# A recurrence over sixteen heads: four groups one after the other, or all keys first and one chain

## The chip, the cores and the metric

The kernel runs on one core of a Trainium2 chip. A core has a matmul engine (PE, with a separate weight load, PEld), a vector engine (DVE), a scalar engine (ACT), a general engine (POOL), a queue engine (SP) and sixteen DMA engines. The engines run side by side; each takes its own instructions in the order in which the built program has them, and waits on semaphores for what others make. Matmuls read SBUF and write PSUM (eight banks of 128 partitions by 512 fp32). The metric is the device time of one execution in microseconds (us): three runs of the kernel before took 1127.19, 1123.43 and 1123.09, median 1123.43.

## The reference

One layer of a hybrid trunk over 512 tokens of width 1024 in fp32. The input is normalized and projected to 11,520 columns, out of which three mixers work:

```
y_a = b_a * causal_dwconv(c_a * x_a)                    # short gated convolution
y_b = rg_lru(causal_dwconv(x_b)) * gelu(g_b)            # linear recurrence, element by element
# RWKV-7: 16 heads of 64, state (64 x 64) per head, over the tokens in order:
state = state * w_t + (state @ -kk_t) (kk_t * a_t)^T + v_t k_t^T
y_t   = state @ r_t
yc    = groupnorm(y) * lnx_g + lnx_b + bonus;  y_c = yc * g_c
m = gate_a * y_a + gate_b * y_b + gate_c * y_c
x = x + m @ w_out;   x = x + relu(rms(x) @ w1)^2 @ w2;   return rms(x)
```

The change concerns the RWKV-7 recurrence and how m is put together; mixers a and b, the projections, the output projection and the MLP compute the same.

## The kernel before, in words

**Matmuls.** Every large product keeps fp32 accuracy by splitting both operands into a rounded part and a rest: mm3 (lines 162 to 165) issues three matmuls of 128x128 against 512 columns (hi x hi, hi x lo, lo x hi). A weight block (128 x 1024) comes by SP's queue into raw (2 buffers); ACT casts it to whi (line 142) and DVE subtracts the rest, wlo (through the helper tt, line 99), each with 3 buffers. One projection is 24 large matmuls, and it needs one such split from DVE.

**The recurrence.** The tokens are cut into 8 chunks of 64, and the 16 heads into 4 groups of 4. For a group:
- krv (385) makes keys, receptances and values from six projections, with some fifteen DVE operations of 512 columns per half group, into AR, BK, v and bv.
- amat (461) makes the masked products of keys inside each chunk: pA matmuls (two of the four heads use the lower 64 rows, two the upper), multiplied by a mask into AXt (DVE, 8 times 512 columns), and transposes of BK (pB).
- inverse (488) inverts the unit triangular matrices of 32 (chunk, head) pairs. DVE transposes AXt into Z, makes 31 steps of two dependent operations (dg<-Z, Z<-Z,dg, 31 to 256 columns on 64 partitions) and transposes back, last into dg. From dg PE makes the off-diagonal blocks (pG, then pT, 32 small matmuls each, with a copy by ACT after each).
- chain (539) carries the state over the chunks. In a chunk: pu = AXt x sv, copied to u0; pu = TT x u0, copied to sv; pS = BKT x sv, which with the old state gives the new one; py = RT x state + AXt x sv, the output, copied to Y. Each step is one 64x64 matmul for each of the group's 4 heads, fp32.
- post (646) and post_norm (609) normalize Y, transpose it (pYt), multiply it by the gate's projection and send it to DRAM (mpd).

**What sets the order.** A scheduler orders every engine's instructions by priority; `tc.high_priority(offset)` moves a piece ahead. weave (752) steps through a critical generator, each piece at the offset CP = 150 (CPI = 60, CPP = 30 where the generator asks for it), and for every step takes r steps of a fill generator. Fill is ab(q) (660), the mixers a and b for 128 of the 1024 channels, eight projections each, and krv of the next group. fill_main (771) lets krv(g + 1) begin only when the inverse of group g is done:

```
        while not GS[g].inv_done:
            yield
        b = krv(g + 1, GS[g + 1])
```

So four times in a row stand: amat and inverse with ab as fill; chain and post with krv of the next group and the rest of ab. The last group's chain has the output projection w_out as fill: w_out(th) for one half of the tokens (256 columns) needs m for that half. pin (167) only keeps matmuls that must not trade places in program order. ab reads the group's y_c back from mpd, adds, splits m into mh and ml and (for six of the eight) sends both to DRAM; open_m fetches them at the end.

After that come the MLP's two products (from line 908), which the change leaves as they are.

## Time and profile before

| | |
|---|---|
| median of three runs | 1123.43 us |
| the profiled execution | 1124.29 us, span 1122.5 us, granted clock 0.986 |
| PE busy | 1086.3 us (97%), 6396 records |
| DVE busy | 762.5 us (68%) |
| ACT busy | 507.5 us (45%) |
| POOL busy | 67.0 us (6%) |
| DMA | 118.8 MB, mean 106 GB/s |

A PE record's duration reaches from its start to the end of its way through the array, so records overlap, and the distance between starts is what one costs. An fp32 matmul is two records. A line number such as L99 or L102 is that of a helper; the names of the tiles tell the operation. The idle time of an engine that nothing waits for costs nothing. A row of the stretches gives the busy time of each engine in a piece of the span.

### The profile page before, as it was taken

To read this page: it belongs to the slowest core of one execution; us is meant where nothing else is said; L and a number is where in the kernel's file an instruction comes from. 1 tells how busy PE (TensorE), PEld (TensorE's weight loads), DVE (VectorE), ACT (ScalarE), POOL (GpSimd) and SP (SyncE) were. 2 spreads that over 40 slices of the span, in tenths; PEclk is the share of its full clock that TensorE was granted. 3 is DMA by queue.
4 is the path that set the end of the run, shared out by engine and by line. 5 is a ranking of instruction groups with operands and counts; after the bars stand their busy time and mean duration, and the time that the engine had idled before them with its cause. 6 is when DMAs were issued, how large, how long until landed. Compare 5 with 4: busy or idle time off the path is not lost.

```text
span 1122.5 us, 16257 instructions
## 1 busy us (share of the span) xinstructions
PE 1086.3 (97%) x6396; PEld 868.4 (77%) x6396; DVE 762.5 (68%) x1367; ACT 507.5 (45%) x826; POOL 67.0 (6%) x108
## 2 busy tenths in 40 slices
PE   8899989999989999989999989999999999999997
PEld 4677867778867778867778867898888888888885
DVE  7998995889975889975888957686444443222224
ACT  6555355534456534466534464555334433111214
POOL 2300000000001000001000020100000000000001
PEclk9899998999999999999999999999999999999999
DMA  6242223231233231233231263454332335333221
GB/s 209 74 122 74 72 85 96 65 114 57 91 118 104 75 118 57 89 115 114 73 109 57 85 189 121 171 175 165 101 104 94 94 94 188 99 104 97 94 94 75
DMA packets 38988, 118.80 MB, mean 106 GB/s; under 512 B 4736, under 2 KB 8320, under 8 KB 38912
## 3 DMA queue, kind: packets, MB, share of 16 engines
q1 hardware_dynamic: 30624, 95.21, 26.7%
q0 software_dynamic: 7568, 21.50, 6.3%
q8 instruction: 50, 0.82, 0.3%
q10 hardware_dynamic: 720, 1.05, 0.3%
q14 instruction: 26, 0.21, 0.1%
HBM read 104.64 MB, written 8.91 MB: 101 GB/s over the span
## 4 chain that ended last, share of the span: by engine, by line
PE 70%; DVE 23%; issue 3%; ACT 2%; DMA 1%; SPq 0%; ACTq 0%; DVEq 0%
PE pp L163 8%; PE pp L165 8%; PE pp L164 8%; PE acc L164 6%; PE acc L165 6%; PE acc L163 6%; PE p L165 5%; PE p L163 5%; PE p L164 5%; DVE wlo L99 5%; DVE dg L99 4%; DVE Z L99 3%; DVE u L102 2%; PE pA L471 2%; DVE g L102 2%
## 5 line engine op out<-in xcount | busy, mean ns | idle before, releaser
L99 DVE TENSOR_TENSOR wlo<-raw,whi 128x1024 fp32r<-128x1024 f32 (+1 forms) x172 | 209.5, 1219 | 216.6 <-ACT whi L142 214.3
L142 ACT CAST whi<-raw 128x1024 fp32r<-128x1024 f32 (+1 forms) x172 | 178.1, 1036 | 284.1 <-PE acc L165 125.1
L165 PE MATMUL pp<-hh,wlo 128*128 128x512 f32 x696 | 278.4, 401 | 5.8 <-DVE wlo L99 5.8
L164 PE MATMUL pp<-hl,whi 128*128 128x512 f32 x696 | 277.5, 399 | 3.2 <-DVE hl L102 3.2
L163 PE MATMUL pp<-hh,whi 128*128 128x512 f32 x696 | 279.3, 402 | 1.4 <-DVE ks L102 0.6
L165 PEld LDWEIGHTS pp<-hh,wlo 128*128 128x128 f32 x696 | 131.9, 190 | 34.8 <-DVE wlo L99 7.4
L163 PEld LDWEIGHTS pp<-hh,whi 128*128 128x128 f32 x696 | 132.1, 190 | 32.2 <-ACT u L664 2.1
L164 PEld LDWEIGHTS pp<-hl,whi 128*128 128x128 f32 x696 | 132.0, 190 | 30.6 <-DVE hl L102 4.3
L165 PE MATMUL p<-h2h,wlo 128*128 128x512 f32 (+1 forms) x264 | 101.2, 383 | 0.0
L163 PE MATMUL p<-h2h,whi 128*128 128x512 f32 (+1 forms) x264 | 101.1, 383 | 0.0
L164 PE MATMUL p<-h2l,whi 128*128 128x512 f32 (+1 forms) x264 | 101.0, 383 | 0.0
L163 PE MATMUL acc<-whi,ah 128*128 128x512 f32 x256 | 99.6, 389 | 0.0
L164 PE MATMUL acc<-wlo,ah 128*128 128x512 f32 x256 | 99.6, 389 | 0.0
L165 PE MATMUL acc<-whi,al 128*128 128x512 f32 x256 | 99.6, 389 | 0.0
L165 PEld LDWEIGHTS p<-h2h,wlo 128*128 128x128 f32 x264 | 49.6, 188 | 9.7
L164 PEld LDWEIGHTS p<-h2l,whi 128*128 128x128 f32 x264 | 49.6, 188 | 9.7
L163 PEld LDWEIGHTS p<-h2h,whi 128*128 128x128 f32 x264 | 49.6, 188 | 9.5
L164 PEld LDWEIGHTS acc<-wlo,ah 128*128 128x128 f32 x256 | 48.0, 188 | 10.1
L165 PEld LDWEIGHTS acc<-whi,al 128*128 128x128 f32 x256 | 48.0, 188 | 10.0
L163 PEld LDWEIGHTS acc<-whi,ah 128*128 128x128 f32 x256 | 48.0, 188 | 9.9
L99 DVE TENSOR_TENSOR Z<-Z,dg 64x31 f32<-64x31 f32 (+15 forms) x124 | 42.2, 340 | 4.1
L99 DVE TENSOR_TENSOR dg<-Z 64x31 f32<-64x31 f32 (+15 forms) x124 | 42.2, 340 | 4.1
(297 smaller groups left out, 1525.0 us busy)
## 6 DMA issues: line engine op xcount, KB each, us to landing
raw<-in_win SPq DMA_DIRECT2D x88, 512.0 KB, 3.5
raw<-in_w SPq DMA_DIRECT2D x64, 512.0 KB, 3.5
raw<-in_wout SPq DMA_DIRECT2D x16, 512.0 KB, 3.5
swr<-in_sw SPq DMA_DIRECT2D x16, 128.0 KB, 2.1
RT<-AR POOLq DMA_DIRECT2D x4, 512.0 KB, 5.4
AXt<-AR POOLq DMA_DIRECT2D x8, 256.0 KB, 5.0
x2T<-in_xt POOLq DMA_DIRECT2D x4, 512.0 KB, 7.1
x2d<-st POOLq DMA_DIRECT2D x8, 256.0 KB, 2.7
```

The costliest lines, as they stand in the source:

```text
L99: return v.tensor_tensor(out=o, in0=a, in1=b, op=op)
L102: return v.scalar_tensor_tensor(out=o, in0=a, scalar=s, in1=b, op0=op0, op1=op1)
L142: ac.copy(hi[:, sl], raw[:, sl])
L163: pe.matmul(ps, wh, xh, start=start, stop=False)
L164: pe.matmul(ps, wh, xl, start=False, stop=False)
L165: pe.matmul(ps, wl, xh, start=False, stop=stop)
L471: pe.matmul(pts[h][:, ci], G_.BK[rows, jj, c], G_.AR[rows, jj, c], start=True, stop=True)
```

## The change

The recurrence is taken in two phases.

**Phase one** goes through the four groups with krv, amat and inverse alone. krv(g) now runs side by side with inverse(g - 1) as one critical stream, with ab(0) to ab(5) as fill (0.60 fill steps to a step). Nothing of a group stays in SBUF for the chain: AR, AXt, BKT, TT and the transposed values are stored by POOL's queue into five DRAM tensors, laid out by chunk (axd, bkd, rtd, ttd, vtd). amat writes to four PSUM banks, the three of the chain and one of pm, and its matmuls alternate between lower and upper rows.

**Phase two** is one chain of eight chunks in which every step has 16 matmuls, for all 16 heads. load_chunk fetches a chunk's operands one chunk ahead (five DMAs on POOL's queue: sv 256 KB, ax 1 MB, tc 256 KB, bk 512 KB, rt 256 KB). The copies between steps are 512 columns wide, one half by DVE and one by ACT. After every second chunk norm treats Y for all heads, 1024 columns at once. Fill is what is left of ab, then gate(q), which prepares for each q a factor GQ and an addend BV such that m = GQ x norm + BV; fin_m applies them to a half of the tokens for all eight q and splits the result, between the gates and w_out(0), and again between w_out(0) and w_out(1). The trips of mh and ml through DRAM are gone. pin now puts all but the first matmul of a step far ahead (HOT = 6000), so that a step's matmuls stand together.

Three places show it, as the program's order has them; the first column is the source line.

PE in the chain before, group 0 (pu, pS and py are the chain's matmuls, pp those of a projection):

```order
L563 MATMUL pu<-sv,AXt 64x64 x4
L165 MATMUL pp<-hh,wlo 128x512
L163 MATMUL pp<-hh,whi 128x512
L164 MATMUL pp<-hl,whi 128x512
L571 MATMUL pu<-u_1554,Z 64x64 x4
L578 MATMUL py<-St,RT 64x64 x4
L165 MATMUL pp<-hh,wlo 128x512
L163 MATMUL pp<-hh,whi 128x512
L593 MATMUL pS<-sv,BKT 64x64 x4
L578 MATMUL py<-sv,AXt 64x64 x4
L164 MATMUL pp<-hl,whi 128x512
```

Each step is four matmuls between two to three large ones.

PE in the chain now, second chunk:

```order
L166 MATMUL pp<-hh,whi 128x512
L632 MATMUL pu<-sv,ax 64x64 x16
L167 MATMUL pp<-hl,whi 128x512
L168 MATMUL pp<-hh,wlo 128x512
L166 MATMUL pp<-hh,whi 128x512
L167 MATMUL pp<-hl,whi 128x512
L168 MATMUL pp<-hh,wlo 128x512
L166 MATMUL pp<-hh,whi 128x512
L167 MATMUL pp<-hl,whi 128x512
L652 MATMUL pu<-u_4737,tc 64x64 x4
L642 MATMUL py<-St,rt 64x64 x16
L652 MATMUL pu<-u_4737,tc 64x64 x12
```

A step's four matmuls have become sixteen, with the projections' matmuls between steps as before.

DVE in the inverse of group 0 before (dg and Z are the inverse's two operations of a step, wlo the weight split):

```order
L99 TENSOR_TENSOR dg<-Z 64x156
L99 TENSOR_TENSOR Z<-Z,dg 64x6x26
L99 TENSOR_TENSOR dg<-Z 64x175
L99 TENSOR_TENSOR Z<-Z,dg 64x7x25
L99 TENSOR_TENSOR dg<-Z 64x192
L99 TENSOR_TENSOR Z<-Z,dg 64x8x24
L99 TENSOR_TENSOR dg<-Z 64x207
L99 TENSOR_TENSOR Z<-Z,dg 64x9x23
L99 TENSOR_TENSOR dg<-Z 64x220
L99 TENSOR_TENSOR Z<-Z,dg 64x10x22
L99 TENSOR_TENSOR wlo<-raw,whi 128x1024
L99 TENSOR_TENSOR dg<-Z 64x231
```

Between the inverse's steps stands a split now and then.

The same place on DVE now (ks, rqw and rqq, a and bl belong to krv of the next group):

```order
L105 SCALAR_TENSOR_TENSOR ks<-pp,part,ks 128x511
L102 TENSOR_TENSOR Z<-Z,dg 64x5x27
L102 TENSOR_TENSOR dg<-Z 64x156
L102 TENSOR_TENSOR Z<-Z,dg 64x6x26
L102 TENSOR_TENSOR dg<-Z 64x175
L102 TENSOR_TENSOR Z<-Z,dg 64x7x25
L102 TENSOR_TENSOR bl<-a_1105,bh 128x512
L102 TENSOR_TENSOR dg<-Z 64x192
L102 TENSOR_TENSOR Z<-Z,dg 64x8x24
L192 STREAM_TRANSPOSE rqw<-pn 128x512
L102 TENSOR_TENSOR wlo<-raw,whi 128x1024
L195 TENSOR_SCALAR rqq<-rqw 128x16
```

The next group's keys have moved in between the same steps.

DVE at the norm of the last chunks before (gst and Y are the norm, x2T and h2l the output projection):

```order
L102 SCALAR_TENSOR_TENSOR gst<-gst 128x8 x2
L99 TENSOR_TENSOR x2T<-acc,x2T 128x256
L99 TENSOR_TENSOR gst<-gst 128x8
L102 SCALAR_TENSOR_TENSOR gst<-gst 128x8 x2
L99 TENSOR_TENSOR gst<-gst 128x8
L102 SCALAR_TENSOR_TENSOR gst<-gst 128x8
L99 TENSOR_TENSOR wlo<-raw,whi 128x1024
L102 SCALAR_TENSOR_TENSOR gst<-gst 128x8
L102 SCALAR_TENSOR_TENSOR h2l<-x2T,part,h2h 128x256
L99 TENSOR_TENSOR Y<-Y,gst 128x512
L99 TENSOR_TENSOR x2T<-acc,x2T 128x256
L99 TENSOR_TENSOR wlo<-raw,whi 128x1024
```

The norm of one group alternates with the output projection's work.

The same place on DVE now:

```order
L102 TENSOR_TENSOR wlo<-raw,whi 128x1024
L691 TENSOR_REDUCE gst<-ysq 128x16
L102 TENSOR_TENSOR wlo<-raw,whi 128x1024
L105 SCALAR_TENSOR_TENSOR h2l<-x2T,part,h2h 128x256
L108 TENSOR_SCALAR gst<-gst 128x16 x2
L102 TENSOR_TENSOR gst<-gst 128x16
L105 SCALAR_TENSOR_TENSOR gst<-gst 128x16 x2
L102 TENSOR_TENSOR gst<-gst 128x16
L105 SCALAR_TENSOR_TENSOR gst<-gst 128x16 x2
L102 TENSOR_TENSOR gst<-gst 128x16
L105 SCALAR_TENSOR_TENSOR gst<-gst 128x16 x2
L102 TENSOR_TENSOR Y<-Y,gst 128x1024
```

The norm's operations are twice as wide and stand closer together.

PE just behind that norm now (pYt are the transposes of Y, acc the output projection):

```order
L166 MATMUL acc<-mh,whi 128x256
L167 MATMUL acc<-ml,whi 128x256
L168 MATMUL acc<-mh,wlo 128x256
L702 MATMUL pYt<-ident,Y 128x128 x8
L166 MATMUL acc<-mh,whi 128x256 x2
L167 MATMUL acc<-ml,whi 128x256
L168 MATMUL acc<-mh,wlo 128x256
L166 MATMUL acc<-mh,whi 128x256
L167 MATMUL acc<-ml,whi 128x256
L168 MATMUL acc<-mh,wlo 128x256
L167 MATMUL acc<-ml,whi 128x256
L168 MATMUL acc<-mh,wlo 128x256
```

The transposes that need the norm stand ahead of the second half of the output projection.

The diff, cut to its core:

```
...
+CP, CPI, CPC, CPN = 150, 60, 70, 5
+HOT = 6000
+R0, R1, R2, R3, R4 = 0.85, 0.60, 1.25, 3.9, 1.0
-HEADS = ((0, 1), (0, 0), (1, 1), (1, 0))
+HEADS = tuple((x, h) for x in range(8) for h in (1, 0))
...
+    def pin(n, mm):
+        if not n:
+            mm()
+            return
+        with tc.high_priority(offset=HOT):
+            m = mm()
+        if m is not None:
+            tc.keep_in_program_order(m)
...
+    def amat(g, G_):
+        G_.AX = p1.tile([P, 2, NC, 4, L], F32, tag="AXt", name="AXt")
+        for c4 in range(2):
+            pts = four_banks("pA")
+            for i in range(16):
+                ci, jj, h = i // 4, i // 2 % 2, i % 2
+                c = 4 * c4 + ci
+                rows = slice(64 * h, 64 * h + 64)
+                pin(i, lambda: pe.matmul(pts[2 * h + jj][:, ci], G_.BK[rows, jj, c], G_.AR[rows, jj, c],
+                                 start=True, stop=True))
+            for e in range(4):
+                tt(G_.AX[:, :, 4 * c4:4 * c4 + 4, e], pts[e].rearrange("p c (a t) -> p a c t", a=2),
+                   mask.rearrange("p (a t) -> p a t", a=2).unsqueeze(2).to_broadcast([P, 2, 4, L]), MUL)
...
+    def load_chunk(c):
...
+        gp.dma_start(flat(sv[64:128]), flat(vtd[c]))
+        gp.dma_start(flat(ax), flat(axd[c]))
+        gp.dma_start(flat(tc_), flat(ttd[c]))
+        if c < NC - 1:
+            gp.dma_start(flat(bk), flat(bkd[c]))
+        if c > 0:
+            gp.dma_start(flat(rt), flat(rtd[c]))
...
+            for n, (x, h) in enumerate(HEADS):
+                g, e = x // 2, 2 * h + x % 2
+                pin(n, lambda: pe.matmul(pu[64 * h:64 * h + 64, x], ax[rows, g, 0, e], sv[rows, g, e],
+                                 start=True, stop=True))
+            u0 = C["ph2"].tile([L, NG, 4, L], F32, tag="u0", name="u0")
+            v.tensor_copy(u0[:, :, 0:2], by_tile(pu[0:64]))
+            ac.copy(u0[:, :, 2:4], by_tile(pu[64:128]))
...
+            if c % 2 == 1:
+                yield CPN
+                norm(c - 1, c + 1)
...
+    def fin_m(c_lo, c_hi):
+        n, th = c_hi - c_lo, c_lo // 4
+        for g in range(NG):
...
+            for h in range(2):
+                q = 2 * g + h
+                y = C["ph2"].tile([P, HT], F32, tag="ym", name="ym", bufs=2)
+                tt(y.rearrange("p (c t) -> p c t", t=L), pt[:, 0:n, 64 * h:64 * h + 64],
+                   GQ[q][th].rearrange("p (c t) -> p c t", t=L), MUL)
+                tt(y, y, BV[q][th], ADD)
+                GQ[q][th], BV[q][th] = gq_tile(q, th, F32R), bv_tile(q, th, F32R)
+                ac.copy(GQ[q][th], y)
+                tt(BV[q][th], y, f(GQ[q][th]), SUB)
...
+    fl = chainit(*[ab(q) for q in range(6)])
+    weave(chainit(krv(0, GS[0]), amat(0, GS[0])), fl, R0)
+    for g in range(1, NG):
+        weave(chainit(side_by_side(krv(g, GS[g]), inverse(g - 1, GS[g - 1])), amat(g, GS[g])), fl, R1)
+    weave(inverse(NG - 1, GS[NG - 1]), fl, R2)
...
+    fc = fill_chain()
+    weave(chain(), fc, R3)
+    weave(end(), fc, R4)
```

More of the change, by code (lines that the diff above doesn't have):

```diff
@@ L382, in block_kernel @@
     class G:
-        inv_done = False
+        pass
     def krv(g, G_):
@@ L525, in inverse @@
             yield
+        for _ in range(NG_T):
+            yield CPI
         for half in range(2):
@@ L834, in last_fill, with fill_chain @@
+    def fill_chain():
+        yield from fl
+        for q in (6, 7):
+            yield from ab(q)
+        for q in range(KT):
+            yield from gate(q)
         wk_ctx.close()
@@ L887, in to_tokens, with end @@
                 yield
-    def post_half(th):
-        yield from post_norm(NG - 1, G_, 4 * th, 4 * th + 4)
-        if th == 0:
-            M["half"] = True
-    fl = last_fill()
-    segments([(chainit(amat(G_), inverse(G_), open_m()), R4),
-              (chainit(chain(G_, 0, 4), post_half(0), chain(G_, 4, NC), post_half(1)), R5)], fl)
-    drain(fl)
-    fin_m(1)
+    def end():
+        while "half" not in M:
+            yield
+        yield from fin_m(4, 8)
+    fc = fill_chain()
+    weave(chain(), fc, R3)
+    weave(end(), fc, R4)
+    drain(fc)
     drain(to_tokens(0))
```

407 lines of the change are left out of this document (176 added, 231 removed).

## The prediction

> **What bounds the kernel now.** I read the page's busy shares first (PE 97%), then cut the span at the marks that the change moves. The stretches below end, in turn, at the last pA matmul of a head group, at its first pG matmul, and so on for four groups (106.8 to 655.4), then at the first matmul of the output projection (703.4) and of the first MLP product (762.8). Columns: length, then busy time and instructions of PE, PEld, DVE, ACT, POOL, granted clock, DMA share, GB/s.
>
> ```profile
> 0.00:106.80 106.80, 97.11 (x408) 71.92 (x409) 91.98 (x176) 62.24 (x94) 18.08 (x26) 0.95 0.39 123
> 106.80:160.10 53.30, 53.30 (x243) 43.50 (x241) 50.49 (x92) 21.57 (x30) 0.56 (x1) 1.00 0.23 74
> 160.10:254.90 94.80, 89.79 (x746) 67.17 (x746) 74.20 (x155) 47.66 (x91) 6.35 (x11) 0.95 0.30 90
> 254.90:338.40 83.50, 79.48 (x347) 64.08 (x345) 73.21 (x119) 42.24 (x61) 2.36 (x6) 0.98 0.31 96
> 338.40:424.30 85.90, 85.48 (x746) 64.21 (x746) 66.32 (x146) 43.11 (x86) 6.82 (x11) 1.00 0.29 90
> 424.30:506.20 81.90, 77.89 (x347) 62.92 (x345) 72.88 (x119) 42.01 (x61) 2.36 (x6) 1.00 0.30 93
> 506.20:592.30 86.10, 86.10 (x749) 64.50 (x748) 66.52 (x147) 42.90 (x86) 6.70 (x10) 1.00 0.30 93
> 592.30:655.40 63.10, 59.49 (x262) 47.85 (x261) 59.04 (x102) 28.27 (x41) 1.72 (x4) 0.97 0.26 81
> 655.40:703.40 48.00, 47.74 (x427) 35.88 (x427) 28.32 (x61) 29.22 (x53) 8.45 (x15) 1.00 0.53 158
> 703.40:762.80 59.40, 59.20 (x561) 55.44 (x561) 45.89 (x98) 33.06 (x66) 5.09 (x8) 1.00 0.54 178
> 762.80:1122.50 359.70, 350.74 (x1578) 290.96 (x1576) 133.65 (x157) 115.22 (x162) 8.55 (x10) 0.99 0.33 107
> sum 1122.50, PE 1086.32 PEld 868.42 DVE 762.51 ACT 507.51 POOL 67.04; mean PE 98.76 PEld 78.95 DVE 69.32 ACT 46.14 POOL 6.09
> ```
>
> PE sets the time almost everywhere; it lacks work for 36 us, 9.7 of them before 106.8 and 9.0 after 762.8, which the change leaves. In the chain stretches (338.4 to 424.3, 506.2 to 592.3) PE never waits. In the inverse stretches (those that end at 160.1, 338.4, 506.2 and 655.4) DVE is busy 88 to 95%, and in the last three PE loses 3.6 to 4 us each; 5 more go right after the first. So two things can be won, PE's own overheads and those waits, and one can be lost: DVE is the engine next in line.
>
> **Fewer runs of small matmuls.** PE's cost of leaving a projection for a run of 64x64 matmuls and coming back:
>
> ```profile
> 204.82 0.39 PE L165 MATMUL pp<-hh,wlo 128*128 128x512 f32 x1
> 205.14 0.45 PE L563 MATMUL pu<-sv,AXt 128*64 128x64 f32 x8
> 205.52 0.50 PE L163 MATMUL pp<-hh,whi 128*128 128x512 f32 x1
> 205.85 0.39 PE L164 MATMUL pp<-hl,whi 128*128 128x512 f32 x1
> 206.08 0.40 PE L165 MATMUL pp<-hh,wlo 128*128 128x512 f32 x1
> ```
>
> A row counts records, two for an fp32 matmul. An undisturbed 128x512 matmul is issued every 0.23 us (205.85 to 206.08). From 204.82 to 205.85 are 1.03 us, of which two such take 0.46 and the eight small records, four matmuls, about 0.28 (the row's 0.45 less most of the pipeline's tail); the remaining 0.3 us is the price of a run. Counted in the order, small matmuls stand in 165 runs before and in 85 after, with as many of each matmul as before. 80 x 0.3 = **24 us of PE time removed**.
>
> **pA in pairs.** The mask products' matmuls use 64 of the 128 rows each. Where the old order happened to alternate the two halves they ran together:
>
> ```profile
> L471 PE MATMUL pA<-AR,BK 64*128 64x128 f32 x256 | 27.9, 285 | 0.9 <-DVE AXt L99 0.8
> 245.88 1.16 PE L471 MATMUL pA<-AR,BK 64*128 64x128 f32 x8
> 248.09 1.49 PE L471 MATMUL pA<-AR,BK 64*128 64x128 f32 x16
> ```
>
> Sixteen records took 0.33 us more than eight. The new order alternates strictly, so at best half of 27.9 goes; some was paired already. I take 11 us (bounds 0 and 14), 2.8 a group. Against it, the four multiplies that free the four banks stand before the second sixteen: about 1 us of wait a group.
>
> **DVE in phase one.** This is the term that decides. The old kernel held krv of the next group back until the inverse was done; now both run together, so DVE's queue between the first transposes of AXt and the last transpose that pG waits for holds far more. Prices:
>
> ```profile
> L99 DVE TENSOR_TENSOR wlo<-raw,whi 128x1024 fp32r<-128x1024 f32 (+1 forms) x172 | 209.5, 1219 | 216.6 <-ACT whi L142 214.3 <-ACT rs L296 1.2
> L99 DVE TENSOR_TENSOR dg<-Z 64x31 f32<-64x31 f32 (+15 forms) x124 | 42.2, 340 | 4.1
> L99 DVE TENSOR_TENSOR AXt<-pA,mask 128x512 f32<-128x512 f32 x32 | 20.9, 686 | 9.3 <-PE pA L471 9.1
> L495 DVE STREAM_TRANSPOSE Z<-AXt 32x1024 f32<-32x1024 f32 x8 | 16.6, 2078 | 0.2
> L517 DVE STREAM_TRANSPOSE dg<-Z 32x1024 f32<-32x1024 f32 x4 | 4.9, 1225 | 0.0
> 729.69 1.22 DVE L99 TENSOR_TENSOR wlo<-raw,whi 128x1024 fp32r<-128x1024 f32 x1
> 730.83 0.68 DVE L618 TENSOR_REDUCE gst<-ysq 128x8 f32<-128x512 f32 x1
> ```
>
> The order of the change has there, for group 0: the 62 operations of the inverse's steps (62 x 0.34 = 21.1), five transposes (4 x 2.08 + 1.2 = 9.5), 11 weight splits (13.4), 48 operations of 512 columns (at 0.7, near the 0.686 of AXt: 33.6), and small change by the same view, 3 scans (3.7), 24 operations of 128x16 (4.1) and one of 256 (0.4): 85.8. An operation that doesn't need its predecessor starts 0.08 before that one's recorded end (729.69 + 1.22 against 730.83); some 80 such neighbours take off 6.4. With the four AXt multiplies ahead (2.7) DVE has **82 us** from the last pA to pG. Groups 1 and 2, counted alike (12 and 10 splits), have 86 and 82.5. PE's work between the same marks is 332, 308 and 330 large matmuls x 0.227 plus 6 to 8 runs and 24 transposes (near a pA record's 27.9 / 256 = 0.11 each): **80, 74 and 79 us**. Before, it was 223 large ones against 6 splits and 13 wide operations. So DVE's queue is now the longer one. Where the two were level before (592.3 to 655.4) each was busy 94% of the stretch. At that share the stretches take 87, 91.5 and 88 us; the lower bound is DVE without a gap (82, 86, 82.5), the upper the 88% that DVE reached in 254.9 to 338.4 (93, 98, 94). I take the 94%, the row of level loads. After pG, up to the next group's last pA, PE leads:
>
> ```profile
> 338.51 2.14 PE pG L522 x64
> ```
>
> 100, 93 and 48 large matmuls, pG and pT (2.14 each), 4 to 5 runs and pA (6.9 less 2.8, plus 1 of wait) make 33, 31.5 and 21 us. The last inverse has 6 splits, 12 wide operations and one of 256 beside its own 30.6: 49 with AXt, against 179 large matmuls (43 with their runs); 50. Up to the first last pA nothing moves but the pairing: 105.5.
>
> Phase one thus ends at 105.5 + 87 + 33 + 91.5 + 31.5 + 88 + 21 + 50 = **507.5 us**, some 40 us (7 + 17.5 + 9 + 7) more than PE's own work would need. The saving on runs is spent on waiting for DVE.
>
> **The chain.** From there to the output projection: 580 large matmuls (131.7), 652 small ones (at some 0.06, a little under the 0.28 / 4 above: 39) in 23 runs (6.9), about 177 in all; the old stretches took 1 to 2% more than such counts give, so 180. The start waits for the last TT to be stored and for the first loads, behind 55 projection matmuls (12.5 us) in PE's order.
>
> ```profile
> x2T<-in_xt POOLq DMA_DIRECT2D x4, 512.0 KB, 7.1
> ```
>
> A store and a 1 MB load after it, each near these 7 us, make 14 and issue time: 2 us late, bounds 0 and 8. Later loads (2.3 MB a chunk, one chunk ahead, over 20 us apart) raise the traffic from about 90 to some 190 GB/s, which the queues carried at a share of 0.54 (178 GB/s in 703.4 to 762.8): hidden by the projections; without that cover each would cost its 7 to 10 us. Chain steps have 7 to 24 large matmuls behind which to hide; I add 2 for chunk 1, where only two stand between py and pu. Sum 184. The copies and the state update shrink DVE's work there, which costs or wins nothing while PE leads.
>
> **The output projection.** The chain now ends inside it. In PE's order 61 matmuls of 256 columns (7.3 us at the 0.12 between the first two rows below) stand between the last py and the transposes pYt that need the norm of the last two chunks. The norm took before, hidden behind other such matmuls:
>
> ```profile
> 728.35 0.28 PE L164 MATMUL acc<-ml,whi 128*128 128x256 f32 x1
> 728.47 0.28 PE L165 MATMUL acc<-mh,wlo 128*128 128x256 f32 x1
> 727.53 0.27 ACT L605 COPY Y<-py 128x128 f32<-128x128 f32 x1 [2.07 <-PE py L578]
> 737.88 0.65 PE L627 MATMUL pYt<-ident,Y 128*128 128x128 f32 x4
> L99 DVE TENSOR_TENSOR x2T<-acc,x2T 128x256 f32<-128x256 f32 x16 | 6.7, 421 | 5.2 <-PE acc L165 4.9
> ```
>
> From Y to pYt is 10.3 us for half the width; four passes of DVE and two of ACT over twice the columns add 3. So 13.3 - 7.3 = 6 us of wait, with all of w_out's second half queued behind pYt. Then fin_m runs for eight heads' tiles, not two: 24 operations of 256 columns (at x2T's 0.42, 10 us), twice, against three weights' 8.6 us of matmuls whose buffers it holds; 3 us each time with the restart. In sum 56.4 of work + 12 = 68.5, against 59.4.
>
> **Sum.** 507.5 + 184 + 68.5 + 359.7 = 1119.7 of span. The profiled execution took 1124.29 for its 1122.5, that is 1.8 more, and the median of the runs is 0.9 below it: **1120.5 us**, 0.3% under before, which is no change: a run of this kernel can't tell less than about 0.5%. Its own range is 1110 to 1130.
>
> **Rivals.**
>
> *DVE keeps up.* If the splits run far enough ahead, or the dependent steps of the inverse fill each other's gaps, PE waits no more than before, and the removed 24 + 11 us stay less the 12 at the end: 1124.3 - 35 + 12 = 1101, **1100** as a median. For it: before, PE waited only 4 us in stretches with DVE at 88%. Against it: the counts above, 82 to 86 against 74 to 80.
>
> *The clock falls.* Slower than before. The waits come in one piece at pG, at the chain's start and at pYt, and PE is granted half its clock after each:
>
> ```profile
> 163.40:168.40 5.00, 0.47 (x3) 0.04 (x1) 4.31 (x6) 4.95 (x8) 1.77 (x3) 0.78 0.40 94
> 168.40:172.00 3.60, 3.57 (x65) 3.51 (x65) 3.48 (x5) 2.53 (x3) 0.00 (x0) 0.50 0.84 231
> 172.00:175.60 3.60, 3.60 (x17) 2.43 (x16) 0.00 (x0) 1.33 (x4) 0.57 (x1) 0.50 0.58 216
> 484.00:488.00 4.00, 1.53 (x7) 0.96 (x6) 3.27 (x5) 0.85 (x2) 0.00 (x0) 1.00 0.38 82
> 488.00:492.00 4.00, 3.78 (x16) 2.86 (x17) 3.21 (x4) 3.28 (x5) 0.00 (x0) 1.00 0.50 167
> ```
>
> After 4.5 us without work the clock stood at 0.50 for 7.2 us, 3.6 lost; after 2.5 us it stayed at 1.00. It decides once gaps in one piece are longer than a point that lies between these two; five of them cost 18: 1120.5 + 18 = **1138.5**. Against it: waits spread over many splits leave the clock alone. The Trainium skill ("TensorE: Matmul & The Clock Gate", Part 1: The HAM clock gate) says that PE falls to half its rate after an idle window of about 3.4 us and needs as long a busy one to return; the trace agrees on the rate (0.50).
>
> **Numbers.** Forecast 0.52 (of it 0.17 under 1117.8, 0.30 within 0.5%, 0.05 over 1129), DVE keeps up 0.25, the clock falls 0.23. Faster 0.42, same 0.30, slower 0.28. The DVE stretches' bounds alone give 1104 to 1139; with the first rival and a little past the second the range is 1100 to 1142.
>
> **What would show it.** 85 runs, and PE free of waits in the chain: the first term. pA busy near 15 us: the second. From last pA to pG near 88 us with DVE at 94% and PE short of work by 6 to 8 us: the third; were PE full there, the first rival holds. A gap of about 6 us before pYt: the last. Wrong altogether if the chain stretch takes much over 184 us (loads late) or the clock's mean falls well under 0.986.

## The result: 3.3% slower

| | before | after |
|---|---|---|
| median beside each other on one chip | 1123.26 us | 1161.15 us (4 runs, 1157.73 to 1165.03) |
| ratio | | 1.033 [1.029, 1.0375] |
| the profiled execution, its span | 1124.29, 1122.5 us | 1160.24, 1158.1 us |
| granted clock | 0.986 | 0.959 |
| PE busy, PE idle | 1086.3, 36.2 us | 1073.4, 84.7 us |
| DVE, ACT, POOL busy | 762.5, 507.5, 67.0 us | 758.3, 484.8, 108.6 us |
| DMA | 118.8 MB | 146.3 MB |

The span grew by 35.6 us: PE is busy 12.9 us less and idle 48.5 us longer. The stretches of the changed kernel, cut at the same marks as in the prediction (the last pA matmul of a group, its first pG, and so on; then the first matmul of the output projection and of the MLP), with the same columns:

```profile
0.00:104.60 104.60, 93.91 (x410) 69.16 (x410) 87.47 (x175) 61.95 (x94) 25.42 (x34) 1.00 0.43 135
104.60:202.10 97.50, 86.58 (x367) 68.78 (x365) 91.60 (x170) 40.32 (x59) 8.91 (x14) 0.93 0.42 115
202.10:233.90 31.80, 31.80 (x286) 26.44 (x286) 16.88 (x24) 15.16 (x20) 2.88 (x5) 1.00 0.37 109
233.90:327.30 93.40, 81.70 (x342) 64.62 (x339) 89.44 (x167) 40.40 (x59) 10.73 (x17) 0.93 0.41 111
327.30:358.30 31.00, 30.34 (x279) 25.08 (x279) 13.40 (x19) 11.23 (x16) 2.05 (x4) 1.00 0.40 120
358.30:463.70 105.40, 86.80 (x365) 68.76 (x363) 91.47 (x169) 42.52 (x62) 11.83 (x18) 0.90 0.39 108
463.70:487.40 23.70, 23.44 (x234) 18.86 (x234) 12.71 (x20) 12.33 (x19) 1.09 (x2) 0.86 0.29 73
487.40:539.90 52.50, 43.23 (x201) 35.43 (x200) 49.63 (x93) 23.80 (x34) 4.66 (x7) 0.95 0.48 132
539.90:730.40 190.50, 187.24 (x1872) 153.72 (x1872) 118.54 (x206) 90.59 (x136) 27.56 (x51) 0.96 0.57 183
730.40:799.40 69.00, 58.34 (x490) 56.12 (x491) 54.25 (x111) 32.25 (x58) 5.44 (x9) 0.90 0.45 149
799.40:1158.10 358.70, 350.01 (x1572) 290.34 (x1570) 132.88 (x157) 114.25 (x159) 8.02 (x9) 0.99 0.33 107
```

The span lies 38.4 us above the predicted 1119.7, and 32.4 of them arise in phase one: it ends at 539.9, and the prediction had 507.5. The four inverse stretches (97.5, 93.4, 105.4, 52.5) hold 10.9, 11.7, 18.6 and 9.3 us without PE, and the granted clock is down in each.

PE's waits of the changed kernel (engine, line, what was waited for: us in total, times, longest):

```profile
PE pA L522 <- DVE BK L102: 13.9, 3, 4.8
PE pp L166 <- DVE ks L105: 10.2, 3, 7.0
PE pG L576 <- DVE dg L571: 9.0, 1, 9.0
PE pYt L702 <- DVE Y L102: 8.6, 1, 8.6
PE pp L166 <- DVE v L105: 5.5, 1, 5.5
PE pn L431 <- ACT bh L161: 3.7, 1, 3.7
```

The line of the same view before that holds its longest single wait:

```profile
PE pT L530 <- ACT dg L524: 4.6, 1, 4.6
```

BK, ks, v and bh belong to krv of the next group, dg is the last transpose of an inverse, Y the last norm. PE waits not only at the ends of DVE's queue, where the prediction looked, but in the middle. One such place in PE's timeline (start, us, operation; in brackets what it waited for):

```profile
175.90 0.49 PE L522 MATMUL pA<-AR,BK 64*128 64x128 f32 x4
180.95 0.79 PE L522 MATMUL pA<-AR,BK 64*128 64x128 f32 x2 [4.56 <-DVE BK L102]
181.68 0.79 PE L168 MATMUL pp<-hh,wlo 128*128 128x512 f32 x1
```

and DVE's at the same time:

```profile
176.11 0.69 DVE L105 SCALAR_TENSOR_TENSOR BK<-a,a 128x512 f32<-128x512 f32 x1
176.72 1.22 DVE L102 TENSOR_TENSOR wlo<-raw,whi 128x1024 fp32r<-128x1024 f32 x1
177.97 0.30 DVE L102 TENSOR_TENSOR Z<-Z,dg 64x135 f32<-64x135 f32 x1
178.29 0.55 DVE L108 TENSOR_SCALAR a<-a,part,dv 128x512 f32<-128x512 f32 x1
178.87 0.27 DVE L102 TENSOR_TENSOR dg<-Z 64x112 f32<-64x112 f32 x1
179.18 0.69 DVE L102 TENSOR_TENSOR a<-a,ks 128x512 f32<-128x512 f32 x1
179.90 0.27 DVE L102 TENSOR_TENSOR Z<-Z,dg 64x112 f32<-64x112 f32 x1
180.21 0.69 DVE L102 TENSOR_TENSOR BK<-a,a 128x512 f32<-128x512 f32 x1
```

The four instructions that make the two BK tiles need 2.6 us; with a weight split and three operations of the inverse between them they take 4.8. PE stands meanwhile, with projections behind pA that need none of this. The clock falls in such a gap (the windows of the ks gap and of what follows it):

```profile
390.40:397.40 7.00, 0.41 (x2) 0.00 (x0) 6.69 (x12) 2.11 (x3) 0.00 (x0) 0.84 0.46 121
397.40:401.00 3.60, 3.17 (x8) 2.50 (x9) 3.44 (x6) 2.62 (x3) 0.00 (x0) 0.50 0.14 22
```

There are eight gaps over 3.5 us, where the kernel before had one of 4.56 (at pT, after the first inverse). The clock fell more often than that: between the first mark and the MLP's first product it fell twelve times, before three times, and it stood at 0.50 for 88.8 us there, before 17.1.

### The profile page after: what moved, and what is told of

The parts are those of the page before. It is cut to its first block, busy times and chain, and to the rows that moved or that the text cites. A ratio compares the mean times of both kernels' runs of the same rounds, so it can differ in the third digit from the quotient of the medians.

```text
span 1158.1 us, 16176 instructions
## 1 busy us (share of the span) xinstructions
PE 1073.4 (93%) x6396; PEld 877.3 (76%) x6396; DVE 758.3 (65%) x1300; ACT 484.8 (42%) x714; POOL 108.6 (9%) x167
## 4 chain that ended last, share of the span: by engine, by line
PE 48%; DVE 4%; DMA 3%; issue 1%; ACT 1%; POOL 0%; ACTq 0%; POOLq 0%; DVEq 0%
PE acc L167 5%; PE acc L166 5%; PE acc L168 5%; PE p L168 5%; PE p L166 5%; PE p L167 5%; PE pp L168 4%; PE pp L167 4%; PE pp L166 4%; DMA raw<-in_wout 1%; PE py L642 1%; ACT whi L145 1%; DVE wlo L102 1%; DMA raw<-in_w 1%; DMA bk<-bkd 1%
## 5 line engine op out<-in xcount | busy, mean ns | idle before, releaser
L166 PE MATMUL pp<-hh,whi 128*128 128x512 f32 x696 | 280.1, 406 | 19.2 <-DVE ks L105 10.2
L167 PE MATMUL pp<-hl,whi 128*128 128x512 f32 x696 | 282.0, 406 | 3.2 <-DVE hl L105 3.2
L168 PE MATMUL pp<-hh,wlo 128*128 128x512 f32 x696 | 281.7, 406 | 1.9 <-DVE wlo L102 1.9
L166 PEld LDWEIGHTS pp<-hh,whi 128*128 128x128 f32 x696 | 135.8, 195 | 52.3 <-DVE ks L105 11.5
L167 PEld LDWEIGHTS pp<-hl,whi 128*128 128x128 f32 x696 | 135.6, 195 | 33.4 <-DVE hl L105 4.0
L168 PEld LDWEIGHTS pp<-hh,wlo 128*128 128x128 f32 x696 | 136.1, 196 | 31.2 <-DVE wlo L102 2.3
## 6 DMA issues: line engine op xcount, KB each, us to landing
bkd<-BKT POOLq DMA_DIRECT2D x4, 1024.0 KB, 13.9
```

The source lines that it names most:

```text
L166: pe.matmul(ps, wh, xh, start=start, stop=False)
L167: pe.matmul(ps, wh, xl, start=False, stop=False)
L168: pe.matmul(ps, wl, xh, start=False, stop=stop)
```

## The experiments

Ratios stand beside runs of the kernel before on the same chip; the 38 us to explain are a ratio of 0.033. D is the theory that DVE has too much to do in phase one, so that the time goes with its load; the rivals (H, L and S in the expectations, each explained where it first stands) say that it is the order in which instructions were put into the engines' queues.

**krv after the inverse again** (all else as changed):

```diff
-weave(chainit(side_by_side(krv(g, ..), inverse(g - 1, ..)), amat(g, ..)), fl, R1)
+weave(inverse(g - 1, ..), fl, RI)                 # RI = 0.90
+weave(chainit(krv(g, ..), amat(g, ..)), fl, RK)   # RK = 0.20
```

> Edit: krv(g) no longer runs beside inverse(g-1); the inverse is issued first, then krv and amat, with the same total of fill (0.90 projections' steps per step of the inverse, 0.20 per step of krv, instead of 0.60 for both). Theory D (DVE's queue holds inverse and krv steps in alternation, so that every result of krv that PE needs comes at half speed): six of the eight PE gaps over 3.5 us (pn 3.7, pA 4.6, 4.6, 4.8, pp 7.0 and 5.5) go, and with each the 3.3 us of half clock behind it; a group's cycle (last pA to last pA) falls from 129, 124 and 129 us to 115 to 119, phase one ends near 510 instead of 540, median near 1128. Theory H (three of the sixteen pA are put early into PE's order and block it, whatever DVE does): pA still stands early here, so its three gaps of 4.6 to 4.8 us stay and the median stays over 1145.

Measured 1148.86, ratio 1.022 [1.019, 1.025]. The waits on BK, ks and v are under 1 us each, and others at pG have come (`pG <- dg` 23.5 us in three, where the change has 9.0 in one). So running the two side by side costs some 12 us, net of those waits; the rest of the 38 stays.

**pA begins with another bank** (the one borrowed from pm, which is free first):

```diff
-ci, jj, h = i // 4, i // 2 % 2, i % 2
+ci, jj, h = i // 4, 1 - i // 2 % 2, 1 - i % 2
```

> Edit: the sixteen pA of a half group begin with the pair that uses the fourth bank (the one that pG, pV and pb also use), so that none of them stands in PE's order ahead of the 50 to 75 projections' matmuls that go before; nothing else moves. Theory H (early pA block PE): the three gaps of 13.9 us and about 3.3 us of half clock behind each go, 24 us: median near 1137. Theory D (DVE is late, PE only shows where): the wait reappears at the next matmuls that need DVE (pb, pV, pG, pp), and the median falls by under 8 us, to 1153 or more.

Measured 1161.36, ratio 1.034 [1.031, 1.0365]. The waits for BK at pA went and came back elsewhere, at pb and at pn (7.5 us in four, where the change has 3.7 in one):

```profile
PE pb L491 <- ACT bh L161: 9.2, 2, 6.0
```

An early pA is a symptom. PE reached the next product of krv sooner and waited there.

**The inverse's steps left out** (30 of 31 in each group, so 240 dependent DVE operations less):

```diff
-for s in range(31):
+for s in range(30, 31):
```

> Leaves out: 30 of the 31 steps of each group's inverse (60 of 62 dependent operations on DVE, some 20 us a group), so the inverse is not computed. Theory D: PE's idle time before the chain falls from about 62 us to under 20, the clock of these stretches rises to 0.98 or more, median 1085 to 1105. Theory H: the early pA still wait for krv's last results; two or three gaps over 3.5 us stay, median over 1115. If neither DVE nor pA is the cause (for instance the store and load traffic, or slower splits), it stays over 1140.

Measured 1105.53 (2 runs), ratio 0.984 [0.980, 0.9875], DVE busy 671.9, PE idle 47.5, clock 0.982. Without these steps the whole loss is gone, and more: 56 us for 86 us of DVE. They are at once load and a dependent chain, which this run can't separate.

**Less fill in the chain**, so that the last norm comes earlier against the output projection:

```diff
-R3 = 3.9
+R3 = 3.4
```

> Edit: 3.4 instead of 3.9 steps of fill for each step of the chain, so that the chain ends some 70 matmuls of projections ahead of the output projection. If the 8.6 us gap before pYt is the norm of the last two chunks with nothing to hide it: the gap goes and the half clock behind it (3.6 us), median near 1149. If the chain needs that cover (rival): its steps wait instead, by as much, and the median stays within 3 us of 1161.

Measured 1160.69, ratio 1.033 [1.030, 1.0365]. The gap of 8.6 before pYt became five of 1.0 to 3.4 (10.3 in sum), and nothing was won, since the clock fell none the less. The first fall came at the end of one gap of 2.5 us, 1.8 us before the next gap began:

```profile
728.87:732.28 3.41, 0.90 (x7) 0.57 (x6) 3.11 (x4) 1.91 (x4) 0.00 (x0) 1.00 0.11 46
732.29:735.70 3.41, 2.41 (x11) 1.93 (x12) 3.38 (x12) 1.51 (x4) 0.80 (x2) 0.50 0.44 154
```

Two more falls followed. In all the clock stood at 0.50 for 13.7 us there, as long as behind the one gap of the change.

**The steps on POOL** (groups 0 to 2):

```diff
-tt(..)
+eng = gp if g < NG - 1 else v
+eng.tensor_tensor(..)
```

> Edit: the 62 dependent operations of the inverse of groups 0 to 2 run on POOL instead of DVE; PE's order around them stays as it was. Theory D (DVE's queue is what PE waits for in phase one): DVE loses 21 us in each of three groups, as in the run without the steps, but for the last group, whose inverse stays on DVE with its 9 us gap: of the 56 us that run gained, about two thirds come back here, median 1115 to 1130, and the gaps on BK, ks, v and bh shrink under 3 us. The price of the steps on POOL is estimated from its 128x512 product (1.3 us): 28 us for the elements plus a start for each, 40 to 45 us a group, which lies inside the 95 us of a stretch. If POOL is slower than that (over 1.3 us a step) PE waits at pG of groups 0 to 2 instead and the median stays over 1145. If it is the alternation as such, and not DVE's load, that delays krv (theory H is already out), the same gain as D is expected; if it is neither, no change.

Measured 1182.28, ratio 1.053 [1.051, 1.055], though DVE's busy time fell by 52 us. A step takes twice as long on POOL, and DVE's own queue stands at the transpose that needs the last one. The group of POOL (busy us, mean ns), and DVE's wait for it:

```profile
L561 POOL TENSOR_TENSOR Z<-Z,dg 64x31 f32<-64x31 f32 (+15 forms) x93 | 66.3, 713 | 6.9
```

```profile
DVE Z L567 <- POOL Z L561: 55.7, 3, 27.7
```

Everything behind that transpose on DVE waited too, and PE with it (25.4 us for krv's rqw, 17.7 for one BK).

**More fill in phase one**: projections of all eight q there, R1 0.75, R2 1.0, R3 2.2.

```diff
-R0, R1, R2, R3, R4 = 0.85, 0.60, 1.25, 3.9, 1.0
+R0, R1, R2, R3, R4 = 0.85, 0.75, 1.00, 2.2, 1.0
-fl = chainit(*[ab(q) for q in range(6)])
+fl = chainit(*[ab(q) for q in range(8)])
```

> Edit: 0.75 instead of 0.60 steps of fill for each step of the groups' inverse and krv, 1.00 instead of 1.25 in the last inverse, 2.2 instead of 3.9 in the chain; the fill of phase one has all eight q, not six. PE then has 1823 instead of 1616 projection matmuls before the last pG (47 us more), DVE some 22 us more with them. If the miss is PE's lack of work beside a DVE that is level with it (D): PE's idle time in phase one falls from 62 us to 35 to 45, phase one ends 25 to 35 us later and the chain stretch is 47 us shorter: median 1135 to 1150. If DVE alone sets phase one, whatever PE has beside it, phase one ends 22 us or so plus the clock's share later with the same idle time in gaps, and if the chain steps lack cover they wait too: median 1155 or more.

Measured 1147.55, ratio 1.023 [1.020, 1.026]; the last pG now waits 11.4 us. The rates and the two more q were worth some 14 us together.

**48 us of independent work off DVE** (the low halves of the 42 weights in the fill are not computed; the high halves stand in):

```diff
 def load_w(..):          # for the fill's names
-    return raw, hi, lo
+    return raw, hi, hi
```

> Leaves out: the low half of the weights of the 42 projections that fill phase one (their split on DVE, 1.22 us each); the third product reads the high half again, so PE's matmuls and their order stay, and the chains of dependent operations (inverse, krv) are untouched. Theory D (DVE's load): DVE loses 51 us, some 45 of them before the last pG; the gaps on BK, ks, v, bh shrink, PE's idle time before the chain falls from 62 us to about 25, the clock there to 0.98: median 1105 to 1120. Rival L (not the load, but the alternation of the inverse's dependent steps with krv and a PE order that expects them sooner): the gaps stay where they are, median over 1145.

Measured 1150.38, ratio 1.021 [1.016, 1.026], DVE busy 710.5. Most of PE's waits stay, some of them shorter:

```profile
PE pA L529 <- DVE BK L103: 8.7, 2, 6.1
...
PE pp L173 <- DVE ks L106: 7.1, 1, 7.1
PE pG L583 <- DVE dg L578: 4.8, 1, 4.8
```

48 us of DVE are worth 11 by the medians (14 by the ratios): D explains little. By this rate the 86 us of the inverse's steps would be worth some 20 as load, an estimate, against the 56 that leaving them out gave.

**krv after the inverse, with the fuller rates** (the first experiment's diff with RI 1.20, R2 1.20, R3 2.2, eight q):

> Edit: the sequential order of the first run with more projections beside the inverse (1.20 instead of 0.90 steps of fill) and 2.2 instead of 3.9 in the chain, the fill of phase one with all eight q. In the sequential run PE waited 10.4, 2.4 and 10.7 us at pG, for DVE with the inverse. Theory D: 3 weights more beside each inverse add 16 us for PE and 8 for DVE there, so PE leads, the waits at pG fall to 2 or 3 us, median 1130 to 1140. If the wait grows with the fill (the splits of the added weights stand in DVE's queue between the inverse's steps and PE waits as long): 1149 or more.

Measured 1148.55, ratio 1.019 [1.015, 1.023]. Only two waits of weight are left, 7.3 us at pYt and this:

```profile
PE pG L577 <- DVE dg L572: 42.8, 4, 11.1
```

Four waits of 10 to 11 us at pG, where the run with less fill had three (23.5 in sum): more fill did not cover them. In the program's order the group's first pG stands ahead of projections that follow it at once; `pin(i, ..)` puts nothing on i = 0, and the kernel before held that very matmul (`pin(i == 0, ..)`). That holding it would remove these four waits is argued here and was not run in this order.

**18 of the 42 splits on POOL:**

```diff
+gp.tensor_tensor(out=w[2], in0=w[0], in1=f(w[1]), op=SUB)   # three weights of each q
```

> Edit: the low half of the weights of 18 of the 42 filling projections is computed on POOL instead of DVE; nothing else changes, PE's order hardly. DVE loses 22 us. By POOL's 128x512 product (1.3 to 1.9 us) a split of 128x1024 takes it 2.6 to 3.8 us, 47 to 68 us in all, on an engine that is 9% busy. Theory D: about 0.4 of the gain of the run that leaves all 42 out, median 1138 to 1146. If the splits come late on POOL (behind its DMA issues, which wait for their data in the same queue) PE waits for wlo instead, median 1161 or more. Rival L: no change, 1158 to 1164.

Measured 1177.49, ratio 1.046 [1.041, 1.050].

```profile
L138 POOL TENSOR_TENSOR wlo<-raw,whi 128x1024 fp32r<-128x1024 f32 x18 | 44.5, 2473 | 156.4 <-ACT whi L137 139.6 <-PE pa L454 16.8
```

2.47 us against DVE's 1.22. The Trainium skill ("GPSIMD Engine Reference", 3.1 Elementwise) gives 1.96 as the ratio for an fp32 two-operand operation; the 2.02 here agrees. The edit took nothing from DVE: its splits fell by 21 us, but its busy time rose from 758.3 to 769.4, since beside 13 of the 18 splits an operation of DVE took 2.2 to 3.6 us, about as long as POOL's split or longer. One of them takes 0.42 us where POOL is idle:

```profile
146.95 2.42 POOL L138 TENSOR_TENSOR wlo<-raw,whi 128x1024 fp32r<-128x1024 f32 x1
146.99 2.67 DVE L103 TENSOR_TENSOR dg<-Z 64x252 f32<-64x252 f32 x1
```

So this run says nothing on theory D; and a late wlo is one more thing PE can stand at (6.1 us in two).

**Each stream its own offset.** In the changed kernel side_by_side hands out the offset that one generator asked for just before it steps the other, so the inverse's 16 waiting steps (offset 60) lowered krv's next steps from 150 to 60, and krv's steps raised the inverse to 150 (the added lines are told in words here):

```diff
-for x_ in list(live):
-    c = next(x_, end)
-    yield c
+# keep [generator, the offset it asked for]
+# and yield that of the one stepped next
```

> Edit: where two generators run side by side, the priority offset that one of them asks for is now used for its own next piece; in the change it goes to the other one's next piece (the inverse's 16 waiting steps lower krv from 150 to 60, and krv's steps raise the inverse and its pG to 150). Theory S (this swap is what delays krv's second half): the gaps on BK, ks and v (14, 10 and 5.5 us) shrink by half or more, median 1140 to 1150. Theory L (the two chains of dependent operations alternate one to one in DVE's queue, whatever the offsets of the waiting steps): the order of the steps themselves is as before, median 1155 to 1164.

Measured 1142.75, ratio 1.017 [1.015, 1.019]: half of the loss back with the same instructions. Waits for BK fell from 13.9 to 6.3, for ks from 10.2 to 2.8, for v from 5.5 to 1.0; those for bh at pn rose from 3.7 to 13.1. One more thing moved with it: the two halves of pT, between which some 80 projection matmuls had stood, came together, so the stretch from pG to the next last pA fell from 31.8 to 16.8 in the first group (and the work went into the stretch ahead of pG):

```profile
203.50:220.30 16.80, 16.80 (x213) 14.02 (x213) 9.84 (x16) 7.56 (x11) 3.82 (x6) 0.90 0.42 105
```

How the 18 us divide between the two was not separated.

**krv ahead of the inverse on DVE** (the inverse's steps ask for an offset of 30, krv's have 150):

```diff
-yield
+yield CPL      # CPL = 30, in inverse's steps
```

> Edit: as in the run on offsets, and the inverse's steps ask for the offset 30 instead of 150, so that on DVE a ready operation of krv always stands ahead of the inverse. DVE's work is the same. Theory L (krv's chain, not DVE's load, is what PE waits for): the gaps on bh, BK, ks and v (46 us with the small ones, and some 18 us of half clock behind them) mostly go; the inverse is later, and up to 10 us of wait appear before each pG, as in the sequential runs: median 1135 to 1148. Theory D (DVE's load): the wait only moves, median 1153 or more.

Measured 1141.10, ratio 1.015 [1.012, 1.0185]: no different from the one above by itself.

**That, and the first pG and pT held in program order**, with eight q and R1 0.65, R2 1.0, R3 2.8:

```diff
-pin(i, ..)            # pG
-pin(i + half, ..)     # pT
+pin(i or -1, ..)
```

> Edit: as the run with krv first; besides, the first pG and pT matmul of each step again may not go ahead of what was issued to PE before it (the kernel before had that rule, the change drops it for the first matmul of a step), the fill of phase one has all eight q (0.65 and 1.00 steps of fill instead of 0.60 and 1.25), and the chain takes 2.8 instead of 3.9. Theory L: both kinds of wait go, PE's idle time before the chain falls from 62 to under 35 us, clock 0.975 or more, median 1105 to 1125. Theory D: 1140 or more.

Measured 1139.97, ratio 1.014 [1.012, 1.016]. The gap at pYt is gone (it was 8.8), but in the run above pG waited only once, in the last group (8.7 us), and it still does (9.3), so this run shows no gain from the held pG. The tuned run below puts more fill ahead of it.

**Own offsets, and the 48 us off DVE** (low halves left out as above):

> Edit: the run with own offsets, and the low half of the 42 filling weights left out as before (its output is wrong by that): DVE loses 48 us, PE's matmuls stay. If DVE's load is what is left of the waits in phase one (D): its 25 to 30 us of gaps there and their half clock go, 1143 falls to 1110 to 1120. If what is left is order at single places, as the first run without these splits suggested (11 us for 48 us of DVE): 1130 or more.

Measured 1132.78, ratio 1.008 [1.006, 1.010]. Again 10 us for 48 of DVE, here mostly pG (9.1 to 1.4).

**Rates set to the repaired order**: R1 0.70, R2 1.5, R3 1.5, the rest as in the run with pG and pT held.

> Edit: as the run with krv first and the first pG and pT held, with 0.70 steps of fill in phase one, 1.5 in the last inverse and 1.5 in the chain: 300 instead of 198 projection matmuls stand ahead of the last pG, and the chain ends ahead of the output projection. If the rest is order at single places: the 9 us before the last pG go with their half clock (12 to 13 us), pYt's stay away, median 1120 to 1128. If the loads are level and the wait only moves: 1136 or more.

Measured 1132.04, ratio 1.008 [1.006, 1.010]; PE idle 66.1, clock 0.978. Neither pG nor pYt is among the longest waits now:

```profile
PE pn L432 <- ACT bh L162: 9.2, 4, 3.1
PE pV L501 <- DVE bv L103: 5.0, 1, 5.0
PE acc L167 <- DVE x2T L103: 4.8, 1, 4.8
```

**The same without krv's precedence** (the inverse at krv's offset, R1 0.72):

> Edit: as the tuned run, but with the inverse's steps at the same offset as krv's and 0.72 steps of fill. If the alternation of krv with the inverse still costs (L), it is 3 to 10 us slower than the tuned run; if only the swapped offsets mattered (S), it is within 2 us of it.

Measured 1145.56, ratio 1.020 [1.018, 1.023]. The alternation of the two streams is worth 13.5 us here, more than was expected; with the rates unset it could not be seen.

**Matmuls of krv held as well**: pb, pV and the first pA kept in program order; then pn too, two fill steps later, with R1 0.66; then, besides, two of krv's operations moved from DVE to ACT.

```diff
+tc.keep_in_program_order(pe.matmul(pb, ..))        # pV and pA alike
+yield; yield; tc.keep_in_program_order(pe.matmul(pn, ..))
+ac.activation(sig, sig, AF.Copy, bias=1.0)         # the last one only, and kp
```

> Edit: the tuned run, and the matmuls pb, the transposes pV and the first pA may not go ahead of what was issued to PE before them; they move back by 45 to 100 projection matmuls. In the tuned run pV and pb wait 5.0, 3.4, 1.6 and 1.4 us. If early places are what is left: these go with part of the half clock, median 1122 to 1128. If DVE's load: the wait reappears at the projections (for a free bank or wlo), median within 3 us of 1132.

> Edit: as the run before it, and pn is held back too, with two more steps of fill ahead of it (0.66 instead of 0.70 steps of fill). In the tuned run pn waits 9.2 us in four places. If early places are what is left: median 1112 to 1122, at or under the kernel before. If DVE's load: within 4 us of 1132, or slower, since krv's chain then starts later.

> Edit: the run that holds all steps back, and two operations of krv for each pair of heads (the addition of one to sig and the product-sum kp, 0.42 and 0.55 to 0.93 us on DVE) run on ACT instead; PE's order is the same. DVE loses 8 to 10 us before the last pG, ACT, which is 42% busy, gains about as much. If DVE's load is what is left (D): half of it or more comes back, median 1119 to 1125, level with the kernel before or under it. If the rest lies elsewhere (the tail, the clock, ACT in krv's chain): 1127 to 1131.

Measured 1132.66 (9 runs, 1125.21 to 1139.24), 1128.98 (10 runs) and 1128.25: ratios 1.008 [1.005, 1.011], 1.0036 [1.001, 1.006] and 1.0032 [1.001, 1.005]. With pn held, the same work, put in another order and with other fill rates, is 32 us faster than the change and still 5 us behind the kernel before; the 5 us that DVE lost to ACT changed nothing. Where these 5 lie is seen by two windows: up to the output projection, and the projection. The version with pn held, then the first of the two for the kernel before (the other stands in the prediction):

```profile
0.00:701.00 701.00, 656.77 (x4401) 525.64 (x4401) 570.68 (x1040) 340.23 (x502) 94.65 (x150) 0.97 0.47 139
701.00:767.60 66.60, 56.86 (x421) 55.28 (x422) 47.44 (x102) 28.20 (x52) 4.89 (x8) 0.88 0.47 151
```

```profile
0.00:703.40 703.40, 676.38 (x4260) 522.02 (x4261) 582.96 (x1113) 359.23 (x600) 53.40 (x90) 0.98 0.32 99
```

Both phases together are 2.4 us shorter than the old four rounds: PE is busy 19.6 us less and idle 17.2 us longer. The output projection is 7.2 us longer, 9.7 of it idle and at a clock of 0.88. No version here beats the kernel before, and whether the two phases can be run without their 44 us of idle PE stays open.

## Why the prediction was wrong

**PE's own savings: right in sum.** The small matmuls stand in 85 runs where there were 165. The clock stood at 0.50 for 94.0 us of the span, and PE was busy in 66.8 of them; before, for 31.3 and 24.2. Half of the difference, some 21 us, is work that took longer. PE is busy 12.9 us less in spite of it: its work became some 34 us shorter, and 24 + 11 were predicted. How the 34 divide between the two terms was not measured. pA's group is at 22.0 us where near 15 was named.

```profile
L522 PE MATMUL pA<-AR,BK 64*128 64x128 f32 x256 | 22.0, 287 | 17.0 <-DVE BK L102 13.9 <-DVE AXt L102 1.8 <-DVE BK L105 0.7
```

The eight long runs of pA did pair: 30 records take 2.05 us and 26 take 1.82, so a record more costs 0.06, about half of the 0.11 from which the prediction started. They make 15.5 of the 22.0; the rest are twelve pieces of two or four records that PE's order put early, each among projections, at 0.5 to 0.8 us.

**DVE's queue: right; the stretches taken from it: wrong.** This is the step that failed. The prediction counted 87, 91.5, 88 and 50 us of DVE from the last pA to the transpose that pG needs. Two of these transposes, and PE's first pG in the same groups (0 and 2):

```profile
192.73 1.23 DVE L571 STREAM_TRANSPOSE dg<-Z 32x1024 f32<-32x1024 f32 x1
447.52 1.22 DVE L571 STREAM_TRANSPOSE dg<-Z 32x1024 f32<-32x1024 f32 x1
```

```profile
202.07 2.11 PE L576 MATMUL pG<-dg,AXt 32*32 32x32 f32 x61
463.70 1.19 PE L576 MATMUL pG<-dg,AXt 32*32 32x32 f32 x32
```

DVE was done 89.4 us after the mark in group 0 (193.96 - 104.6) and 90.4 in group 2 (448.74 - 358.3); in groups 1 and 3 93.0 and 52.3. All four are within 2.5 us of the count. But PE came to pG 8 and 15 us after DVE. "DVE's queue is now the longer one" took a stretch as the longer of two queues that meet at its end. They meet some ten times on the way, at each product of krv that PE makes from what DVE or ACT prepared and at each return, and both are in order: PE's 80 us of work, plus 11 to 19 us of standing at those places, plus the half clock behind the longer ones (97.5 x 0.07 = 7 and 105.4 x 0.10 = 11 us), made 97.5 and 105.4 (a part of the clock's loss falls inside the waits). The experiments agree: the same work in another order and with other fill rates gave 32 us back (18 of them with the offsets alone), and 48 us less load in the same order 11. These two stretches are 28 of the 38 us that the span lay above the sum.

The term that the sum put at nothing is the clock. The sum stood on 1086.3 - 35 = 1051.3 us of busy PE and so on 68.4 us without; measured were 1073.4 and 84.7. Of the 38 us, then, 22 are a longer busy time, nearly all of it the 21 us of work at half the clock, and 16 are more standing. The prediction's own sign that it would be wrong altogether, a mean clock well under 0.986, is what came: 0.959. That the stretch of group 1 came out near its number (93.4 for 91.5) is in part luck: it stood 11.7 us where 17.5 were in the count, and its clock was 0.93.

**The clock rival held the right mechanism, and too small a size.** It put five gaps at 18 us beside the predicted waits; there were twelve falls where before had three, most of them not at the places it named, and they took 44.4 us (half of 88.8), 3.7 each, near the 3.6 it took. Its rule, that the length of a gap in one piece decides, does not hold: the clock fell with no gap over 2.0 us as well (the last section has the rows). The prediction argued against this rival that waits spread over many splits leave the clock alone; most waits were not spread, they stood in pieces of 4 to 9 us at krv's products, and of those that were, two took the clock down too. "DVE keeps up" fell: it is what leaving the steps out looks like, 1105.5.

**From pG to the next pA**: 31.8, 31.0 and 23.7, predicted 33, 31.5 and 21. Right; that pT's halves were kept apart by 80 matmuls (pin(i + half) holds the second half's first one behind all that was issued) was not seen, and cost nothing in these stretches themselves.

**The chain**: 190.5 where 184 stood. The loads were on time, with 1.9 us of waits for one (bk). The excess is the clock of its first 20 us after the 9.0 us at pG, granted 0.70:

```profile
539.90:560.00 20.10, 20.10 (x174) 17.11 (x175) 8.21 (x12) 6.65 (x9) 5.61 (x10) 0.70 0.43 125
```

which is 6 us lost. **The output projection** took 69.0 of the predicted 68.5, with a gap of 8.6 where 6 was named; since its clock was 0.90, which the count did not have, the match is in part luck. **The rest** took 358.7, predicted 359.7.

## What to carry to other kernels

Two in-order queues that exchange operands many times do not take the longer of the two: count the meetings, ask at each which side is late by the instructions put between a producer's parts, and price the half clock, some 3.7 us here for each fall, wherever PE works little for some 3.4 us. When a change makes two streams run side by side, look first at what fixes the order within the queues (which matmul is held, whose offset a step gets, how much fill stands beside it): here that was worth 32 us, and taking 48 us of load off the busy engine 10 or 11.

## What the runs showed of the hardware

The clock followed stretches of about 3.4 us and not the length of one gap. In the changed kernel's trace it stands at 0.50 for 3.41 us or a multiple of it (6.83, 13.66, 17.07). Of the twelve falls between the first mark and the MLP eleven came at the end of a stretch of 3.41 us in which PE was busy for 1.52 us or less, one of them with no gap over 1.9 us:

```profile
255.17:258.58 3.41, 1.52 (x7) 0.98 (x6) 3.22 (x7) 1.63 (x2) 0.00 (x0) 1.00 0.32 77
258.58:261.99 3.41, 3.41 (x10) 2.66 (x9) 3.22 (x7) 0.00 (x0) 1.02 (x3) 0.50 0.55 154
```

In the run with less fill in the chain one gap of 2.5 us left 0.90 us of work in such a stretch, and the clock fell. In the kernel before a gap of 2.46 us lay across the ends of two stretches, which left 1.68 us in the first, and the clock stayed:

```profile
483.67:487.08 3.41, 1.68 (x8) 1.06 (x6) 3.40 (x4) 0.00 (x0) 0.16 (x1) 1.00 0.24 77
```

So a gap of about 2.5 us can cost the half clock or nothing. The Trainium skill ("TensorE: Matmul & The Clock Gate", Part 1: The HAM clock gate) has a free-running window of about 3.4 us, and a clock that halves after one idle window; the lengths and the 0.50 agree, but the windows here that counted as idle were busy for up to 1.52 of 3.41 us. The twelfth fall is not explained by this: ahead of 466.80 PE had been busy for the whole stretch, for most of it with the 32x32 matmuls of pG.

Work given to POOL cost twice what it did on DVE, in small steps (0.65 to 0.71 us against 0.34) and in large ones (2.47 against 1.22), and where DVE needed its result the whole of DVE's queue stood, up to 27.7 us at once. Beside most of POOL's 2.4 us splits an operation of DVE took as long as the split (2.67 us for one of 0.42).

Half-array matmuls in strict alternation paired inside a run (0.06 us a record, against 0.11); those that the order left alone in twos and fours did not, and cost 0.5 us or more a piece.
